# Six tiles instead of three held back at the stage borders of a two-block network, their weights kept in activation slots, and score products grouped by height

## The chip, the cores and the metric

One core of one Trainium2 chip runs the whole kernel in one launch. The metric is the device time in microseconds (us) of one execution; the lower the better. An engine's matmul is TensorE (PE); elementwise work lies on VectorE (DVE), ScalarE (ACT) and GpSimd (POOL); loads are issued on SyncE's queue (SP).

## The reference

The reference runs a first block of two layers (a mixer, attention to a memory, a convolutional feed-forward) on 512 tokens of width 1024, and then a second block of two layers. The change touches the second block only:

```python
for i in range(DEPTH):                       # layer 0 has a context stream of 256 tokens, layer 1 uses it only as input
    h  = modulate(rmsnorm(x, norm_mix_w[i]), sh_m, sc_m)
    hc = modulate(rmsnorm(ctx, norm_mix_w[i]), shc_m, scc_m)
    y, y_c = ab_mixer(h, hc, ...) if i % 2 == 0 else cd_mixer(h, hc, ...)
    x = x + g_m * y
    x = x + g_f * swiglu(modulate(rmsnorm(x, norm_ffn_w[i]), sh_f, sc_f), w_gate[i], w_up[i], w_down[i])
    if not last:
        ctx = ctx + gc_m * y_c
        ctx = ctx + gc_f * swiglu(modulate(rmsnorm(ctx, norm_ffn_w[i]), shc_f, scc_f), ...)
return rmsnorm(x, final_norm_w)
```

Here `modulate(h, shift, scale)` is `h * (1 + scale) + shift`. `cd_mixer` joins a Fourier mix with a gated linear attention of 4 heads that runs forward and backward over the tokens.

## The kernel before

Activations lie feature-major: a tile has 128 features by 512 tokens (256 for the context), eight tiles make the width of 1024. Every fp32 product is made of three products of reduced type: high weight by high activation, high by low, low by high. `unit` (L287 to L295) loads 128x1024 raw weights on SP (`wr`, 4 buffers), casts the high half on ACT (L293, `wh`, 3 buffers) and subtracts the low half on DVE (L294, `wl`, 3 buffers). Activations, squares and other working tiles come from one pool A of 66 slots through `T()`; PSUM has a pool for projections (`pm`, 4 banks) and one for the rest (`pa`, 4 banks).

The instructions are written down in program order, and a scheduler makes each engine's queue from that.

`gated` (L1421 on) is the output projection of a stage. For each of eight tiles m it takes the weights, makes x of the tile (three matmuls per 128 of depth), evacuates with gate and residual on DVE (L1428), and calls `stat_add` (L419 on): ACT squares the tile into a fresh slot of A (L423), and POOL adds it to a running sum (L428; DVE for the last tile). With a context it does the same with 256 tokens (evacuation L1438). Two things are held back at the border to the next stage, to give PE work there:

- `defer=3`: the context part of the last three tiles becomes six jobs (each half the depth). This is at border A (`w_abo`, layer 0 mixer to swiglu) and B (the third part of `w_dn0` to `cd_mixer`).
- `halves=3`: the last three x tiles are made in two halves of 256 tokens; the second halves become three jobs. This is at border C (`w_cdo` to swiglu, layer 1) and D (the third part of `w_dn1` to `final_norm`). Depth is 4 tiles of 128 at A and C, 6 at B and D.

The next stage runs the jobs and advances `modulate` between them: first the column sum of the squares (L417 on PE, L436 on DVE, L411 on POOL), later the broadcast (L480 on PE, L1089 on ACT). When all jobs have run, the eight tiles are modulated (L1102 on DVE, L1103 on ACT, L1110 on DVE; for three of them L1098 on POOL, L1099 and L1100 on ACT, L1108 on DVE), and the next projection begins (L1169, L1158). `cd_mixer` clears tiles by memset (L1549).

In `head` (L1758 on), for each of four heads and either direction, four score blocks are made of two products each: one of 128 rows (L1786, ZK by ZQ) and one of 64 rows (L1787, Z2), one after the other into the same block; a predicated copy then takes the bank of that direction. Other small products of the head have 64 rows too (L1774, L1776). A full fp32 product of 128 columns shows as two records.

Of the kernel before, what the change touches and what calls it, by code (L numbers as in the profile page):

```python
# [8 lines left out]
F32R = mybir.dt.float32r  # L9
# [141 lines left out]
def layout(i):  # L151
    a = {}
    a["x"] = fm_act(i["x"][0])
    a["mem"] = fm_act(i["mem"][0])
    v = {}
    for l in range(2):
        v[f"mixg{l}"] = cols(i["mix_norm_g"][l])
        v[f"xag{l}"] = cols(i["xa_norm_g"][l])
        v[f"xmg{l}"] = cols(i["xa_mem_norm_g"][l])
        v[f"ffg{l}"] = cols(i["ffn_norm_g"][l])  # L160
        v[f"xaq{l}"] = cols(i["xa_q_norm_g"][l])
        v[f"xak{l}"] = cols(i["xa_k_norm_g"][l])
        v[f"cw{l}"] = cols(i["ffn_conv_w"][l])
        v[f"cb{l}"] = cols(i["ffn_conv_b"][l])
        v[f"nm{l}"] = cols(i["norm_mix_w_2"][l])
        v[f"nf{l}"] = cols(i["norm_ffn_w_2"][l])
        v[f"ab{l}"] = cols(i["ada_b_2"][l])
    v["retg"] = cols(i["ev_ret_norm_g"][0])
    v["hgg"] = cols(i["ev_hg_norm_g"][0])
    v["lb"] = cols(i["hg_lb_logits"])  # L170
    v["odq"] = cols(i["od_q_norm_g"][0])
    v["odk"] = cols(i["od_k_norm_g"][0])
    v["nfin"] = cols(i["final_norm_w_2"])
    v["sgn"] = cols(i["ab_sgu_norm_w_2"][0])
    v["c"] = cols(i["c_2"][0])
    v["cc"] = cols(i["c_ctx_2"])
    v["dbf"] = cols(i["cd_decay_b_fwd_2"][0])
    v["dbb"] = cols(i["cd_decay_b_bwd_2"][0])
    v["hn"] = cols(i["cd_head_norm_w_2"][0])
    a["vec"] = np.ascontiguousarray(np.concatenate([v[n] for n, _ in VEC], axis=1))  # L180
    w = i["ev_w_in"][0]
    a["w_ev"] = fm_units(np.concatenate([w[:, 0:1024], w[:, 1536:3072], w[:, 3584:4096]], axis=1))
    a["w_evt"] = tm_units(np.concatenate([w[:, 1024:1536], w[:, 3072:3584]], axis=1))
    a["w_evo"] = fm_units(i["ev_w_out"][0])
    for l in range(2):
        a[f"w_xq{l}"] = fm_units(i["xa_w_q"][l])
        a[f"w_xk{l}"] = fm_units(i["xa_w_kv"][l][:, 0:1024])
        a[f"w_xv{l}"] = tm_units(i["xa_w_kv"][l][:, 1024:2048])
        a[f"w_xo{l}"] = fm_units(i["xa_w_o"][l])
        a[f"w_fi{l}"] = fm_units(i["ffn_w_in"][l])  # L190
        a[f"w_fo{l}"] = fm_units3(i["ffn_w_out"][l])
    a["w_od"] = fm_units(i["od_w_in"][0][:, 0:2048])
    a["w_odt"] = tm_units(i["od_w_in"][0][:, 2048:3072])
    a["w_odo"] = fm_units(i["od_w_out"][0])
    a["ctx"] = fm_act(i["ctx_2"][0])
    w = i["ab_w_in_2"][0]
    a["w_ab"] = fm_units(np.concatenate([w[:, 0:512], w[:, 1024:2048]], axis=1))
    a["w_abt"] = tm_units(np.concatenate([w[:, 512:1024], w[:, 2048:2560]], axis=1))
    a["w_abo"] = fm_units(i["ab_w_out_2"][0], 4)
    a["sguw"] = np.ascontiguousarray(i["ab_sgu_w_2"][0].transpose(2, 0, 1))  # L200
    a["sgub"] = np.ascontiguousarray(np.broadcast_to(i["ab_sgu_b_2"][0][None], (128, 4, 128)))
    q = np.arange(128)
    rel = np.arange(48) - 16
    ri = np.arange(8)[None, :, None] - (q // 16)[:, None, None] + 7
    ci = np.clip(rel[None, None, :] - (q % 16)[:, None, None] + 15, 0, 30)
    a["nab"] = np.ascontiguousarray(i["ab_rel_bias_2"][0][:, ri, ci].transpose(1, 0, 2, 3)).reshape(128, 8, 384)
    for l in range(2):
        a[f"w_gu{l}"] = fm_units(np.concatenate([i["ffn_w_gate_2"][l], i["ffn_w_up_2"][l]], axis=1))
        a[f"w_dn{l}"] = fm_units3(i["ffn_w_down_2"][l])
    a["w_ada"] = np.ascontiguousarray(i["ada_w_2"].reshape(2, 8, 128, 6, 2, 512).transpose(0, 3, 4, 1, 2, 5))  # L210
    w = i["cd_w_in_2"][0]
    z = np.zeros((1024, 16), np.float32)
    wa = np.concatenate([w[:, 2048:2064], z, w[:, 2064:2080], z, z, z, z, z], axis=1)
    a["w_cd"] = fm_units(np.concatenate([w[:, 512:1024], w[:, 1536:2048], wa, w[:, 0:512]], axis=1))
    a["w_cdt"] = tm_units(w[:, 1024:1536])
    a["w_cdo"] = fm_units(i["cd_w_out_2"][0], 4)
    dw = np.zeros((64, 512), np.float32)
    dw[0:16, 0:256], dw[16, 0:256] = i["cd_decay_w_fwd_2"][0], i["cd_decay_b_fwd_2"][0]
    dw[32:48, 256:512], dw[48, 256:512] = i["cd_decay_w_bwd_2"][0], i["cd_decay_b_bwd_2"][0]
    a["decw"] = dw  # L220
    dist = np.arange(128)[:, None] + 384 - np.arange(512)[None, :]
    a["odb"] = np.ascontiguousarray(i["rel_bias"][t5_bucket(dist)].transpose(2, 0, 1))
    return a


class Net:
# [917 lines left out]
    def wt(self, w, u, kt=8):  # L1144
        self.tick()
        return self.unit(self.a[w][u][:, 0:kt * 128])

    def dx(self, wt, xs, n=512, ps=None, s=None, ks=None):

        nc = self.nc  # L1150
        if ps is None:
            ps = self.PM()
        s = s or slice(0, n)
        last = len(xs) - 1
        for j in ks or range(last + 1):
            (xh, xl), ws = xs[j], slice(j * 128, j * 128 + 128)
            for i, (A, B) in enumerate(((wt[0], xh), (wt[0], xl), (wt[1], xh))):
                nc.tensor.matmul(ps[:, s], A[:, ws], B[:, s], start=j == 0 and i == 0, stop=j == last and i == 2)  # L1158
        return ps
# [87 lines left out]
    def ab_mixer(self, x, st, c, cs):  # L1247
        nc, a = self.nc, self.a
# [167 lines left out]
        jobs += [lambda m=m: out_part(m) for m in range(8)]  # L1416
        self.weave(units(), jobs, depth=4, rate=0.85)
        self.side = side
        return self.gated("w_abo", lambda m: 2 * m + 1, bx, bc, part, part_c, 0, 2, defer=3)

    def gated(self, w, u, yx, yc, x, c, l, j, defer=0, halves=0, stats=True):  # L1421

# [20 lines left out]
        whole = slice(0, 512)  # L1443
        held = []
        for m in range(8):
            wt = self.wt(w, u(m), len(yx))
            t = self.xp.tile([128, 512], F32, tag="x", name=f"x{self.n}") if m < 8 - halves else x[m]
            r["x"].append(t)
            if m < 8 - halves:
                ev_x(m, self.dx(wt, yx), t, whole)  # L1450
                if stats and halves:
                    for h, st in enumerate((r["sx"], r["sx2"])):
                        self.stat_add(st, m, t[:, h * 256:h * 256 + 256], 256)
                elif stats:
                    self.stat_add(r["sx"], m, t)
            else:
                held.append((m, wt, self.PM(), t))
            if yc:
                if m < 8 - defer:
                    self.run(part_c(m, wt))  # L1460
# [3 lines left out]
        for h, st in enumerate((r["sx"], r["sx2"])):  # L1464
            s = slice(h * 256, h * 256 + 256)

            def half(i, s=s, st=st):
                m, wt, ps, t = held[i]
                self.dx(wt, yx, 256, ps, s)
                ev_x(m, ps, t, s)  # L1470
                if stats:
                    self.stat_add(st, m, t[:, s], 256)

# [7 lines left out]
    def swiglu(self, l, r):  # L1481
# [9 lines left out]
            mx = self.modulate(x, r["sx"], l, 3, 0, xs, 256, H[0])  # L1491
        for i, job in enumerate(r["jobs"]):
            job()
            if i in ((2, 3) if c else (1, 2)):
                next(mx, None)
        self.run(mx)
        late = self.modulate(c, r["sc"], l, 3, 1, cs, 256, self.CS) if c else self.modulate(x, r["sx2"], l, 3, 0, xs, 256, H[1])
# [28 lines left out]
        for p, (lo, hi) in enumerate(PARTS):  # L1526
            for j in range(len(hx), min(hi + 1, 22)):
                gate_up(j)
            last = p == 2
            r = self.gated(f"w_dn{l}", lambda m: 3 * m + p, hx[lo:hi], hc[lo:hi], x, c, l, 5,  # L1530
                           defer=3 if last and c else 0, halves=3 if last and not c else 0, stats=last)
            x, c = r["x"], r["c"]
        return r

    def cd_mixer(self, r):
# [3 lines left out]
        mx = self.modulate(x, r["sx"], 1, 0, 0, xs)  # L1539
        for i, job in enumerate(r["jobs"]):  # L1540
            job()
            if i in (2, 3):
                next(mx, None)
        self.run(mx)
        SCf, SCb = self.T(), self.T()
# [211 lines left out]
        def head(h):  # L1757
# [20 lines left out]
            nc.scalar.copy(O1, p1)  # L1778
            nc.scalar.copy(O2[0], p2[0])
            nc.scalar.copy(O2[1], p2[1])  # L1780
            for d, SC in ((0, SCf), (1, SCb)):
                ZQ, ZK = Z[d]
                ps = self.PA()
                for j in range(4):
                    s = slice(j * 128, j * 128 + 128)
                    nc.tensor.matmul(ps[:, s], ZK[:, s], ZQ[:, s], start=True, stop=False)  # L1786
                    nc.tensor.matmul(ps[:, s], Z2[d][1][P, s], Z2[d][0][P, s], start=False, stop=True)  # L1787
                nc.vector.copy_predicated(SC.rearrange("p (b t) -> p b t", t=128), glm[:, d].bitcast(I32).unsqueeze(1).to_broadcast([128, 4, 128]),
                                          ps.rearrange("p (b t) -> p b t", t=128))
            SC = self.T()  # L1790
            nc.vector.tensor_add(SC, SCf, SCb)
            yield
# [44 lines left out]
            jobs += steps(f_out(g)) * 2  # L1837
        jobs += [lambda m=m: out_part(m) for m in range(8)]
        self.weave([head(0), head(1), decayed(1, 0), decayed(1, 1), head(2), head(3)], jobs, depth=2, rate=1.0)
        return self.gated("w_cdo", lambda m: 2 * m + 1, ys[4:8], None, part, None, 1, 2, halves=3)  # L1840

    def final_norm(self, r):
        nc = self.nc
# [20 lines left out]
                nc.sync.dma_start(self.a["out"][:, 2 * k:2 * k + 2, s], out[k].rearrange("p (k t) -> p k t", k=2))  # L1864

        first, second = half(0, r["sx"], 3), half(1, r["sx2"], 2)
        for job in r["jobs"]:
            job()
            next(first)
            if job is r["jobs"][1]:  # L1870
                break
        r["jobs"][2]()
        next(second)
        self.run(first, second)

# [123 lines left out]
```

## Time and profile before

| | |
|---|---|
| time of three runs, us | 3155.07, 3155.63, 3159.87 (median 3155.63) |
| the profiled execution, us | 3161.09 |
| its span, first to last instruction, us | 3159.3 |
| PE busy, us (share of the span) | 3102.5 (98%) |
| DVE, ACT, POOL busy, us | 1779.6, 1118.1, 436.7 |
| mean granted clock of TensorE | 0.991 |

The span is what the profile covers; the profiled execution has 1.8 us more around it. The share of busy time tells which engine has no room; the list of waits tells for what PE stood still; a timeline gives start, duration, engine, line and operation, and in brackets the idle time before and what ended it. The granted clock is given in windows as a share of full speed.

### The profile page before, as it was taken

How to read it: one execution, taken by the hardware profiler on the slowest of the kernel's cores; microseconds unless marked ns; L12 is line 12 of the kernel's file. 1: busy time of each engine (PE TensorE's matmuls, PEld its weight loads, DVE VectorE, ACT ScalarE, POOL GpSimd, SP SyncE). 2: the span in 40 equal slices, each digit the busy share in tenths (PEclk: the TensorE clock that was granted, in tenths of full speed). 3: DMA queues.
4: the chain of work that ended last, by engine and by line, in shares of the span. 5: the costliest groups of instructions: out<-in, count | busy, mean ns of one | idle time of the engine just before them, and what ended most of it. 6: DMA issues, size and time to landing. Idle time of an engine off the chain costs nothing. (4 is left out here: it accounts for less than half of the span.)

```text
span 3159.3 us, 40998 instructions
## 1 busy us (share of the span) xinstructions
PE 3102.5 (98%) x16292; PEld 2590.3 (82%) x16292; DVE 1779.6 (56%) x2894; ACT 1118.1 (35%) x1859; POOL 436.7 (14%) x375
## 2 busy tenths in 40 slices
PE   8999999999999999999999999999999999999998
PEld 6878888888877888888878778888888877788887
DVE  7767676575658857768654467342322453543333
ACT  2225353232445544423343545211212452342222
POOL 5023111010112111101121112000000310120001
PEclk9999999999999999999999999999999999999999
DMA  4224323333323423334342013232211220132222
GB/s 170 78 76 155 115 84 117 117 120 122 128 94 112 144 77 113 121 124 162 129 146 93 23 40 119 96 105 85 78 67 51 89 80 31 36 102 95 99 96 72
DMA packets 110355, 312.80 MB, mean 99 GB/s; under 512 B 12178, under 2 KB 17683, under 8 KB 110163
## 3 DMA queue, kind: packets, MB, share of 16 engines
q1 hardware_dynamic: 101968, 297.32, 27.7%
q10 hardware_dynamic: 8194, 12.86, 1.3%
q8 instruction: 128, 2.10, 0.3%
q14 instruction: 65, 0.52, 0.1%
HBM read 306.98 MB, written 3.15 MB: 98 GB/s over the span
## 5 line engine op out<-in xcount | busy, mean ns | idle before, releaser
L1158 PE MATMUL m<-t,wh 128*128 128x512 f32 (+1 forms) x4124 | 1093.0, 353 | 1.1 <-DVE t L1110 0.4
L293 ACT CAST wh<-wr 128x1024 fp32r<-128x1024 f32 (+2 forms) x485 | 487.8, 1008 | 1244.2 <-PE m L1158 422.2
L294 DVE TENSOR_TENSOR wl<-wr,wh 128x1024 fp32r<-128x1024 f32 (+2 forms) x485 | 579.2, 1195 | 450.1 <-ACT wh L293 438.3
L1158 PEld LDWEIGHTS m<-t,wh 128*128 128x128 f32 x4124 | 726.3, 190 | 115.3 <-issue 11.6
L312 PE MATMUL m<-t,wh 128*128 128x512 f32 (+1 forms) x2576 | 772.9, 383 | 0.0
L1158 PE MATMUL m<-t,wl 128*128 128x512 f32 (+1 forms) x2062 | 724.8, 352 | 0.5 <-DVE wl L294 0.5
L312 PEld LDWEIGHTS m<-t,wh 128*128 128x128 f32 x2576 | 474.1, 188 | 89.8 <-issue 1.0
L312 PE MATMUL m<-t,wl 128*128 128x512 f32 (+1 forms) x1288 | 491.5, 382 | 0.0
L1158 PEld LDWEIGHTS m<-t,wl 128*128 128x128 f32 x2062 | 390.8, 190 | 52.7 <-issue 1.9
L312 PEld LDWEIGHTS m<-t,wl 128*128 128x128 f32 x1288 | 242.7, 188 | 46.2 <-issue 0.7
L428 POOL TENSOR_TENSOR t<-t,t 128x512 f32<-128x512 f32 (+1 forms) x90 | 115.8, 1293 | 1162.8 <-ACT t L423 1162.4
L1062 DVE SCALAR_TENSOR_TENSOR t<-t,silc,t 128x512 f32<-128x512 f32 x280 | 219.0, 810 | 16.5 <-DMA t<-w_ada 15.8
L939 PE MATMUL m<-t,wh 128*128 128x512 f32 x704 | 217.3, 390 | 0.0
L342 PE MATMUL m<-t,wh 128*128 128x512 f32 x496 | 160.1, 402 | 7.3 <-ACT wh L293 7.3
L939 PEld LDWEIGHTS m<-t,wh 128*128 128x128 f32 x704 | 131.9, 188 | 27.2
L906 POOL TENSOR_TENSOR t<-t,t 128x512 f32<-128x512 f32 x44 | 64.5, 1465 | 549.8 <-ACT t L905 540.2
L401 ACT CAST t<-t 128x512 fp32r<-128x512 f32 x116 | 72.0, 621 | 189.0 <-DVE t L1520 104.0
L939 PE MATMUL m<-t,wl 128*128 128x512 f32 x352 | 137.1, 389 | 0.0
L1428 DVE SCALAR_TENSOR_TENSOR x<-m,modt,x 128x512 f32<-128x512 f32 (+1 forms) x70 | 49.3, 705 | 154.2 <-PE m L1158 154.1
L411 POOL TENSOR_TENSOR s<-s,nh 128x4 f32<-128x4 f32 (+2 forms) x67 | 72.1, 1078 | 439.3 <-DVE s L471 161.3
L357 PE MATMUL m<-wh,t 128*128 128x512 f32 x384 | 123.2, 397 | 0.0
L342 PEld LDWEIGHTS m<-t,wh 128*128 128x128 f32 x496 | 93.6, 192 | 26.7 <-ACT wh L293 8.0
(387 smaller groups left out, 3405.7 us busy)
## 6 DMA issues: line engine op xcount, KB each, us to landing
t<-w_ada SPq DMA_DIRECT2D x192, 256.0 KB, 4.0
wr<-w_fi SPq DMA_DIRECT2D x88, 512.0 KB, 3.3
wr<-w_gu SPq DMA_DIRECT2D x88, 512.0 KB, 3.3
wr<-w_fo SPq DMA_DIRECT2D x32, 512.0 KB, 3.4
wr<-w_dn SPq DMA_DIRECT2D x32, 512.0 KB, 3.2
wr<-w_ev SPq DMA_DIRECT2D x24, 512.0 KB, 3.3
wr<-w_xk SPq DMA_DIRECT2D x16, 512.0 KB, 3.4
wr<-w_xv SPq DMA_DIRECT2D x16, 512.0 KB, 3.4
```

Source lines behind the costliest of these rows:

```text
L293: nc.scalar.copy(h[:, 0:e], r[:, 0:e])
L294: nc.vector.tensor_sub(lo[:, 0:e], r[:, 0:e], h[:, 0:e])
L312: nc.tensor.matmul(ps[:, 0:n], A[:, s], B[:, 0:n], start=c == 0, stop=c == tot - 1)
L342: self.nc.tensor.matmul(ps, A[:, s], B, start=k == 0 and i == 0, stop=k == K - 1 and i == 2)
L357: nc.tensor.matmul(pss[tb], A[:, ts], B[:, s], start=(u == 0 and j == 0 and i == 0), stop=(u == nu - 1 and j == kper - 1 and i == 2))
L401: nc.scalar.copy(h[:, 0:n], src[:, 0:n])
L411: self.nc.gpsimd.tensor_tensor(r, v, self.nh[:, 0:w], ALU.pow)
L428: e.tensor_tensor(st[0][:, 0:n], st[0][:, 0:n], sq[:, 0:n], ALU.add)
L906: nc.gpsimd.tensor_tensor(y, y, rb, ALU.mult)
L939: nc.tensor.matmul(ps[:, 0:n], A[:, s], B[:, 0:n], start=c == 0, stop=c == tot - 1)
L1062: nc.vector.scalar_tensor_tensor(acc[i], r, s, acc[i], ALU.mult, ALU.add)
L1158: nc.tensor.matmul(ps[:, s], A[:, ws], B[:, s], start=j == 0 and i == 0, stop=j == last and i == 2)
```

## The change

- A class `Wide` joins several 512-wide pieces into one weight. `wt_kept` is a second way to take a weight: it casts and subtracts in pieces of 512 columns, high and low half of each piece into slots of A.
- In `gated`, tiles from 8 - max(defer, halves) on take their weights by `wt_kept`; held tiles no longer take a PSUM bank ahead.
- `defer` and `halves` rise from 3 to 6 (to 5 at border D); the places at which `modulate` is advanced between the jobs move back; `final_norm` advances its first half behind the first two jobs, runs the other three, and then takes the second half's statistics.
- In `head`, all products of 64 rows of both directions come first, then all of 128 rows, and then both copies; both PSUM banks are open meanwhile. Only a bank's first product starts it.

```diff
+class Wide:
+    def __init__(self, tiles):
+        self.tiles = tiles
+    def __getitem__(self, key):
+        s, o = key[1], key[1].start // 512
+        return self.tiles[o][key[0], s.start - o * 512:s.stop - o * 512]
...
+    def wt_kept(self, w, u, kt):
+        nc = self.nc
+        self.tick()
+        r = self.raw(self.a[w][u][:, 0:kt * 128])
+        hs, los = [], []
+        for o in range(0, kt * 128, 512):
+            n = min(512, kt * 128 - o)
+            h, lo = self.T(F32R), self.T(F32R)
+            nc.scalar.copy(h[:, 0:n], r[:, o:o + n])
+            nc.vector.tensor_sub(lo[:, 0:n], r[:, o:o + n], h[:, 0:n])
+            hs.append(h)
+            los.append(lo)
+        return Wide(hs), Wide(los)
...
-        return self.gated("w_abo", lambda m: 2 * m + 1, bx, bc, part, part_c, 0, 2, defer=3)
+        return self.gated("w_abo", lambda m: 2 * m + 1, bx, bc, part, part_c, 0, 2, defer=6)
...
         for m in range(8):
-            wt = self.wt(w, u(m), len(yx))
+            kept = m >= 8 - max(defer, halves)
+            wt = (self.wt_kept if kept else self.wt)(w, u(m), len(yx))
...
-                held.append((m, wt, self.PM(), t))
+                held.append((m, wt, t))
...
             def half(i, s=s, st=st):
-                m, wt, ps, t = held[i]
-                self.dx(wt, yx, 256, ps, s)
-                ev_x(m, ps, t, s)
+                m, wt, t = held[i]
+                ev_x(m, self.dx(wt, yx, 256, None, s), t, s)
...
-            if i in ((2, 3) if c else (1, 2)):
+            if i in ((4, 8) if c else (1, 3)):
                 next(mx, None)
...
-                           defer=3 if last and c else 0, halves=3 if last and not c else 0, stats=last)
+                           defer=6 if last and c else 0, halves=5 if last and not c else 0, stats=last)
...
-            if i in (2, 3):
+            if i in (2, 5):
                 next(mx, None)
...
-            for d, SC in ((0, SCf), (1, SCb)):
-                ZQ, ZK = Z[d]
-                ps = self.PA()
+            pss = [self.PA(), self.PA()]
+            for d in range(2):
                 for j in range(4):
                     s = slice(j * 128, j * 128 + 128)
-                    nc.tensor.matmul(ps[:, s], ZK[:, s], ZQ[:, s], start=True, stop=False)
-                    nc.tensor.matmul(ps[:, s], Z2[d][1][P, s], Z2[d][0][P, s], start=False, stop=True)
+                    nc.tensor.matmul(pss[d][:, s], Z2[d][1][P, s], Z2[d][0][P, s], start=j == 0, stop=False)
+            for d in range(2):
+                ZQ, ZK = Z[d]
+                for j in range(4):
+                    s = slice(j * 128, j * 128 + 128)
+                    nc.tensor.matmul(pss[d][:, s], ZK[:, s], ZQ[:, s], start=False, stop=j == 3)
+            for d, SC in ((0, SCf), (1, SCb)):
...
-        return self.gated("w_cdo", lambda m: 2 * m + 1, ys[4:8], None, part, None, 1, 2, halves=3)
+        return self.gated("w_cdo", lambda m: 2 * m + 1, ys[4:8], None, part, None, 1, 2, halves=6)
...
-        for job in r["jobs"]:
+        for i, job in enumerate(r["jobs"]):
             job()
-            next(first)
-            if job is r["jobs"][1]:
-                break
-        r["jobs"][2]()
+            if i < 2:
+                next(first)
         next(second)
```

## Rows read from the trace of the kernel before

**Rows 1.** The profile page: PE's busy time, share of the span and instructions, and the granted clock in 40 slices, in tenths of full speed (9 is 90% or more); last a group of DMA issues: name, instructions, KB each, median us from issue to landing.
```profile
PE 3102.5 (98%) x16292; PEld 2590.3 (82%) x16292; DVE 1779.6 (56%) x2894; ACT 1118.1 (35%) x1859; POOL 436.7 (14%) x375
...
PEclk9999999999999999999999999999999999999999
...
wr<-w_gu SPq DMA_DIRECT2D x88, 512.0 KB, 3.3
```

**Rows 2.** PE's waits: the waiting line and what released it, us in total, times, the longest.
```profile
PE a L417 <- DVE t L428: 11.3, 6, 2.5
...
PE a L480 <- POOL s L411: 7.1, 11, 1.3
```

**Rows 3.** Timeline of all engines at border A: start us, duration us, engine, line, operation, in brackets the idle time before and its releaser.
```profile
1930.73 0.63 ACT L423 ACTIVATE t<-x 128x512 f32<-128x512 f32 x1 [2.09 <-DVE x L1428]
...
1931.51 1.28 POOL L428 TENSOR_TENSOR t<-t,t 128x512 f32<-128x512 f32 x1 [1.43 <-ACT t L423]
...
1932.46 0.40 PE L1158 MATMUL m<-t,wh 128*128 128x256 f32 x2
...
1932.67 0.75 DVE L1428 SCALAR_TENSOR_TENSOR x<-m,modt,x 128x512 f32<-128x512 f32 x1 [1.97 <-PE m L1158]
...
1933.45 0.63 ACT L423 ACTIVATE t<-x 128x512 f32<-128x512 f32 x1 [2.09 <-DVE x L1428]
...
1937.96 0.65 PE L480 MATMUL a<-ident,s 128*128 128x128 f32 x4 [0.19 <-POOL s L411]
...
1941.17 0.98 PE L417 MATMUL a<-c,t 128*128 128x1 f32 x4 [2.32 <-DVE t L428]
```

**Rows 4.** Timeline of all engines at border B, columns as in the group before.
```profile
2496.43 0.65 PE L480 MATMUL a<-ident,s 128*128 128x128 f32 x4 [0.77 <-POOL s L411]
...
2498.91 0.48 DVE L1438 SCALAR_TENSOR_TENSOR c<-m,modt,c 128x256 f32<-128x256 f32 x1 [1.34 <-PE m L1158]
2499.31 0.74 DVE L1102 SCALAR_TENSOR_TENSOR t<-x,modt,a 128x512 f32<-128x512 f32 x1
2499.79 0.41 ACT L423 ACTIVATE t<-c 128x256 f32<-128x256 f32 x1
...
2500.87 0.58 PE L417 MATMUL a<-c,t 128*128 128x1 f32 x4 [2.00 <-DVE t L428]
...
2502.01 0.71 POOL L411 TENSOR_TENSOR s<-s,nh 128x2 f32<-128x2 f32 x1 [2.61 <-DVE s L436]
...
2502.77 0.43 PE L480 MATMUL a<-ident,s 128*128 128x128 f32 x2 [0.52 <-POOL s L411]
...
2506.02 4.73 POOL L1549 MEMSET t<- 128x512 f32 x10
```

**Rows 5.** Timeline of all engines at border C.
```profile
2779.13 0.43 PE L480 MATMUL a<-ident,s 128*128 128x128 f32 x2 [1.25 <-POOL s L411]
...
2781.83 0.99 PE L417 MATMUL a<-c,t 128*128 128x1 f32 x4 [2.27 <-DVE t L428]
...
2783.86 0.69 PE L480 MATMUL a<-ident,s 128*128 128x128 f32 x2 [1.04 <-POOL s L411]
```

**Rows 6.** Windows (from:to, length, then busy us and instructions of PE, PEld, DVE, ACT, POOL; then the granted clock, the share of the DMA engines and GB/s).
```profile
1940.50:1942.50 2.00, 1.33 (x5) 1.36 (x6) 1.87 (x4) 1.93 (x3) 0.15 (x2) 0.51 0.28 111
1942.50:1947.00 4.50, 4.50 (x13) 3.34 (x12) 4.50 (x6) 2.86 (x5) 3.99 (x3) 0.50 0.78 264
...
2503.80:2507.00 3.20, 3.20 (x9) 2.43 (x9) 3.20 (x4) 2.55 (x4) 3.20 (x5) 0.50 0.24 96
...
2780.20:2787.00 6.80, 4.13 (x19) 4.08 (x20) 4.64 (x12) 3.99 (x9) 3.71 (x5) 0.50 0.41 147
```

**Rows 7.** The chain of work that ended last, through the first pair of heads: start us, us, engine, bank, line and issues.
```profile
2643.80 0.64 PE a L1774 x4
...
2645.30 0.45 PE a L1774 x4
...
2646.61 0.42 PE a L1786 x2
2647.03 0.41 PE a L1787 x2
```

**Rows 8.** Timeline of all engines ahead of border C.
```profile
2765.94 0.62 ACT L293 CAST wh<-wr 128x512 fp32r<-128x512 f32 x1 [1.02 <-issue]
2766.13 0.75 DVE L1428 SCALAR_TENSOR_TENSOR x<-m,modt,x 128x512 f32<-128x512 f32 x1 [1.37 <-PE m L1158]
...
2766.91 0.73 ACT L423 ACTIVATE t<-x 128x256 f32<-128x256 f32 x2 [0.35 <-DVE x L1428]
```

**Rows 9.** The 512-wide cast of a weight (groups by line and shape: busy us, mean ns of one, idle before), and from the timeline of all engines ahead of border A the subtraction of the low half, first alone, then beside POOL's additions.
```profile
L293 ACT CAST wh<-wr 128x512 fp32r<-128x512 f32 x32 | 19.8, 620 | 48.4 <-PE m L1158 39.1 <-issue 9.3
...
1908.82 0.69 DVE L294 TENSOR_TENSOR wl<-wr,wh 128x512 fp32r<-128x512 f32 x1
...
1916.25 2.44 POOL L428 TENSOR_TENSOR t<-t,t 128x512 f32<-128x512 f32 x2 [1.81 <-ACT t L423]
...
1916.69 1.40 DVE L294 TENSOR_TENSOR wl<-wr,wh 128x512 fp32r<-128x512 f32 x1
```

**Rows 10.** The chain of work that ended last: a dense stretch of 96 matmuls of 512 columns, and one of 18 matmuls of 256 columns.
```profile
2622.04 21.76 PE m L1158 x96
...
3146.30 2.15 PE m L1158 x18
```

More of the change, by code (lines that the diff above doesn't have):

```diff
@@ L1780, in head @@
             nc.scalar.copy(O2[1], p2[1])
-            for d, SC in ((0, SCf), (1, SCb)):
-                ZQ, ZK = Z[d]
-                ps = self.PA()
+            pss = [self.PA(), self.PA()]
+            for d in range(2):
                 for j in range(4):
                     s = slice(j * 128, j * 128 + 128)
-                    nc.tensor.matmul(ps[:, s], ZK[:, s], ZQ[:, s], start=True, stop=False)
-                    nc.tensor.matmul(ps[:, s], Z2[d][1][P, s], Z2[d][0][P, s], start=False, stop=True)
+                    nc.tensor.matmul(pss[d][:, s], Z2[d][1][P, s], Z2[d][0][P, s], start=j == 0, stop=False)
[5 more added lines that the diff above has]
+            for d, SC in ((0, SCf), (1, SCb)):
                 nc.vector.copy_predicated(SC.rearrange("p (b t) -> p b t", t=128), glm[:, d].bitcast(I32).unsqueeze(1).to_broadcast([128, 4, 128]),
-                                          ps.rearrange("p (b t) -> p b t", t=128))
+                                          pss[d].rearrange("p (b t) -> p b t", t=128))
             SC = self.T()
```

## The prediction, made blind

> **What bounds the kernel now.** I read the profile page first: TensorE (PE) is busy 98% of the span and the line of granted clocks shows full speed in all 40 slices [rows 1]. So a change pays only where it shortens PE's own work or one of its few waits. The list of PE's waits says where these are [rows 2]: most for the column sum L417 after the addition of squares L428 (11.3 us in 6 waits), 7.1 us for the broadcast L480 after POOL's rsqrt. These are the stage borders. Third I read the timelines of the borders, called A (mixer to swiglu, layer 0), B (swiglu to cd_mixer), C (cd_mixer to swiglu) and D (the end). At A, PE waits 0.19 us at L480 and 2.32 at L417 [rows 3]; at B 0.77, 2.00 and 0.52 [rows 4]; at C 1.25, 2.27 and 1.04 [rows 5]. Fourth, the windows: the granted clock is 0.50 (the 1.2 GHz level) in 4.5, 3.2 and 4.13 busy us behind A, B and C [rows 6]; half of each is lost, 2.25, 1.6 and 2.1 us. Last the chain through the score products [rows 7].
>
> **In which order tiles are written.** The step that decides is the change's choice of place: the kept weights are cast into slots of the activation pool A, which also holds the squares of L423. Now a weight has pools of its own and its cast runs ahead: at C the 512-wide cast L293 starts at 2765.94, before the evacuation L1428 (2766.13) and the square (2766.91) of an earlier tile [rows 8]. Slots of A, by contrast, seem to be written first in the program's order. At B the broadcast was ready at 2497.08 and DVE idled 1.34 us, yet the first modulate L1102 starts at 2499.31, only behind the last deferred L1438; the memsets L1549, which read nothing, start at 2506.02, though POOL had no work for 2.61 us before its L411 at 2502.01 [rows 4]. I take it that this order holds for the new casts too. In the changed program the square of tile m is written before the weights of tile m+1. At A and B the cast of each kept x tile then waits for the square of the tile before, that for its evacuation, that for the last matmul: no weight is prefetched across tiles. The held tiles become six, and PE stands still ahead of each.
>
> **Parts at A and B.** From the end of PE's last issue for a tile to the evacuation 0.21 us (1932.46 to 1932.67), to the square 0.78, the square 0.63 [rows 3], the 512-wide cast 0.62 [rows 9], a hand-over of some 0.05 (an estimate): 2.3 us. Two matmuls with the high half follow (0.454 us at 21.76/96 = 0.227 each [rows 10]); the third needs the low half. Its subtraction takes 0.69 alone, but 1.40 beside POOL's addition of squares [rows 9]; that starts 0.15 us behind the square [rows 3] and lasts 1.2 to 1.3, so it lies beside most of the subtraction. The excess over the 0.454 is 0.28 to 1.0, and I take 0.8, nearer the second row: 3.1 us a tile. The first kept tile follows a context tile (0.48 and 0.41 us in place of 0.75 and 0.63 [rows 3, 4]): 2.6. Border A: 5 x 3.1 + 2.6 = 18.1; B the same, since its second, narrower piece is cast beside the first's matmuls. Together **+36.2 us**, from 2 x (5 x 2.58 + 2.1) = 30.0 to 2 x (5 x 3.3 + 2.8) = 38.6.
>
> Behind the waiting casts ACT has only later casts and that tile's square, DVE the subtraction and the next evacuation, and nobody else needs them. The raw loads on SP keep their number and order, but a raw buffer comes free one tile later and the next stage's loads with it; twelve deferred context jobs (six issues of 0.12 us each at A, nine at B [rows 10]) cover these, and without that cover a load would cost up to its time to landing, 3.3 us [rows 1]. The casts in pieces cost a little more ACT and DVE time, off the path.
>
> **What the borders give back.** Twelve jobs instead of six, with the broadcast four or five jobs after the sum, cover the waits at L480 (0.19 and 0.77). The end stays: the last context square still goes through L428 and L417 behind the last job, and the modulate cannot pass the last L1438. Of the waits of 2.0 to 2.3 us there I count half as filled by modulate work that stands ready earlier: -1.6 at A, -1.3 at B, **-2.9**. Bounds: nothing, and all of them (0.19 + 2.32 + 0.77 + 2.00 + 0.52 = 5.8).
>
> **C and D.** Here all held weights are cast one behind the other, with no square between them, so there is one stall each of 3.0 us (before the first held tile); the three more tiles in halves at C and two at D cost, per matmul, 2.15/18 = 0.119 instead of 0.227/2 [rows 10], 0.4 us more at either border. At C the six second halves cover most of the three waits (4.56): -3.4, from 0 to -4.6. C sums to **0**, D to +3.0 + 0.4 - 0.2 = **+3.2**: its tail, the last stat, rsqrt and store, has the same steps as before.
>
> **Score products.** Now 64-row and 128-row products alternate. Two L1786 issues take 0.42 us, two L1787 0.41; four L1774 behind a 64-row group take 0.45, so two 0.225; behind a 128-row group 0.64 [rows 7]. Each change of height costs 0.19. Per pair of heads there are 34 changes now (one in, 32 between products, one out), four after: 30 x 0.19 = 5.8, and for two pairs **-11.5 us**, from -9 (some of it back in waits for the later copy) to -12. The second PSUM bank is held a little longer; the 16 products of a head together take 16 x 0.225 = 3.6 us, no wait for a bank is in the rows, so I cost it at nothing.
>
> **The clock.** Twelve stalls of about 3 us between 2.7 us (A, 12 matmuls) and 4.1 us (B, 18) of work. At A the clock fell to 0.51 in a stretch that holds the wait of 2.32 [rows 3, 6], so these stalls can do it as well. One low stretch cost 1.6 to 2.25, mean 2.0: 12 x 2.0 = 24, less 0.45 for each stall, since two slow matmuls cover more of the subtraction: **+18 us**. Bounds: nothing, and every kept matmul at the half level, 6 x 2.7 + 6 x 4.1 - 5.4 = 35. The Trainium skill (TensorE: Matmul & The Clock Gate, HAM oscillation) names a length of gap below which the array should keep its clock; by it none of these stalls would lower it and the sum would stay at 25. The row at A speaks against: its wait was shorter than these and the clock fell.
>
> **Sum**: 36.2 - 2.9 + 0 + 3.2 - 11.5 = +25.0, and 18 of clock: +43. The profiled execution took 3161.1 us (span 3159.3, 1.8 around it), 5.5 above the median of the runs, so it would be 3204; from the median, 3155.6 + 43 = **3199 us**.
>
> **The rivals.** (1) Ends on the other side: the casts run ahead as today. Its place is the order of first writes in A; from the point where a cast may start before the square of the tile before, there is no stall at A to D. Then the borders give back their waits with the low clock behind them: A 2.3 + 2.25, B 3.3 + 1.6, C 4.0 less 0.4, D about 0.3 lost; with the heads -11.5 that is 24 us faster: **3131**. For it: the slots are not scarce, and nothing in the data makes a cast wait. Against: the memsets and the modulate at B. Chance 0.10. (2) Gated, but stalls at the lower bound and no loss of clock: 30.0 - 2.9 + 3.2 - 11.5 = 18.8: **3174**; for it that the granted clock is full in nearly all of the kernel. Chance 0.14. (3) Gated, and the clock stays low through all kept tiles: 25 + 35 = 60: **3216**; for it that stall follows stall with less than 4.1 us of work between them. Chance 0.16. (4) The change does little, stalls and gains in balance, for instance if only the gated cast but not the subtraction is waited for and ACT is early: within 6 us of before, 0.03. My forecast, between 3185 and 3210, has 0.57.
>
> **How the numbers follow.** What a measurement can tell from no change is 0.2%, 6.3 us. Only rival 1 is faster by more: 0.10. Same 0.03, slower 0.87. The range leaves out rival 1 and the outer edge of rival 3, and takes in rival 2 with a smaller stall: 3166 to 3222.
>
> **What would show it.** In the changed profile: at A and B each first matmul of a kept tile waits for a cast or a subtraction of `wt_kept`, about 2.3 to 3.3 us, six times each; each such cast starts as the square of the tile before ends; a granted clock well under 1 in both stretches. PE's waits at L480 gone at A and B, the last L417 still there. L1786 and L1787 in their new grouping at 0.11 us an issue. One stall of about 3 us at C and at D. I am wrong if casts of `wt_kept` start before the squares of the earlier tile, or if PE's idle time at A and B does not rise by some 30 us; then rival 1 holds and the time is below 3145.

## The result and the profile after

The changed kernel takes 3207.39 us (median of four runs, 3201.94 to 3208.2) against 3157.75 for the kernel before: ratio 1.0149, 95% interval 1.0136 to 1.0162, so 47 us slower (about 43 to 51); the two medians differ by 49.6, and the median of the kernel before now includes a fourth run of 3160.95 us. The forecast was 3199 in a range of 3166 to 3222. The profiled execution took 3206.59 us with a span of 3204.8.

Line numbers have moved: the evacuation L1428 is now L1453, the square L423 is L433, the addition L428 is L438, the column sum L417 is L427, the broadcast L480 is L490, the projection L1158 is L1183. The new casts of kept weights are L1167, their subtractions L1168. First the page, PE's busy time and the granted clock in 40 slices [rows 1], then the list of PE's waits [rows 2]: waiting line and releaser, us in total, times, longest.

```profile
PE 3115.4 (97%) x16364; PEld 2600.6 (81%) x16364; DVE 1788.5 (56%) x2910; ACT 1118.9 (35%) x1870; POOL 432.4 (13%) x375
...
PEclk9999999999999999999999998999999899999999
```

```profile
PE m L1183 <- ACT t L1167: 27.4, 14, 2.1
PE a L427 <- DVE t L438: 10.0, 7, 2.5
PE m L1183 <- DVE t L1168: 8.7, 13, 1.9
...
PE a L490 <- POOL s L421: 4.9, 9, 1.2
```

Two new waits stand in the list, on the casts and on the subtractions of kept weights: 36.1 us together. The old ones have become less by only 1.3 and 2.2 us (11.3 to 10.0, 7.1 to 4.9). Now the timeline of all engines at border A, one kept tile to the next:

```profile
1915.62 0.75 DVE L1453 SCALAR_TENSOR_TENSOR x<-m,modt,x 128x512 f32<-128x512 f32 x1 [2.00 <-PE m L1183]
1916.40 0.63 ACT L433 ACTIVATE t<-x 128x512 f32<-128x512 f32 x1 [4.57 <-DVE x L1453]
1916.94 0.60 ACT L1167 CAST t<-wr 128x512 fp32r<-128x512 f32 x1
1917.17 1.27 POOL L438 TENSOR_TENSOR t<-t,t 128x512 f32<-128x512 f32 x1 [4.76 <-ACT t L433]
1917.57 1.43 DVE L1168 TENSOR_TENSOR t<-wr,t 128x512 fp32r<-128x512 f32 x1 [1.20 <-ACT t L1167]
1917.59 0.73 PE L1183 MATMUL m<-t,t 128*128 128x512 f32 x2 [2.01 <-ACT t L1167]
...
1919.05 4.14 PE L1183 MATMUL m<-t,t 128*128 128x512 f32 x10 [0.73 <-DVE t L1168]
```

This is the chain that was forecast, step by step: evacuation, square, cast right behind the square, PE after 2.01 us of standing still; two matmuls; then 0.73 us more for the subtraction, which takes 1.43 us beside POOL's addition, against 0.69 alone [rows 9]. The Trainium skill (SBUF — State Buffer, Who interferes with whom) says that a VectorE instruction with two SBUF inputs contends with a GpSimd instruction that reads SBUF; the trace agrees, 1.43 against 0.69. The ten matmuls behind it take 4.14 us where 2.27 would be dense (10 x 0.227 [rows 10]): the clock is low, 0.75 of full speed on average over the kept tiles of A (a window of that stretch stands below, at the run with three kept tiles). At B the same, with one subtraction later still because it stands in DVE's queue behind two of the next stage's:

```profile
2500.53 0.73 PE L1183 MATMUL m<-t,t 128*128 128x512 f32 x2 [2.01 <-ACT t L1167]
2502.00 5.54 PE L1183 MATMUL m<-t,t 128*128 128x512 f32 x16 [0.73 <-DVE t L1168]
...
2522.50 6.01 PE L1183 MATMUL m<-t,t 128*128 128x512 f32 x16 [1.91 <-DVE t L1168]
```

To see where the time went, the kernel is cut at instructions that both kernels have: stage A from the last cast (L1350, now L1375) of layer 0's attention to its eighth gate activation of the swiglu; B from the last such activation to the first gate of `cd_mixer`; C, with the heads in it, from the last of these gates to the eighth activation of layer 1's swiglu; D from the last activation to the end. Between the stages both kernels take the same time to 0.02 us. Windows A, B, D and C of the kernel before (columns as in [rows 6]):

```profile
1905.19:2067.62 162.43, 159.92 (x914) 140.29 (x915) 87.69 (x130) 55.94 (x93) 23.65 (x20) 0.98 0.29 103
2435.36:2629.65 194.29, 188.01 (x957) 155.32 (x956) 94.12 (x157) 83.18 (x126) 43.30 (x45) 0.96 0.23 78
3109.61:3159.30 49.69, 39.87 (x232) 35.03 (x230) 20.15 (x35) 15.00 (x32) 14.21 (x19) 0.93 0.19 67
...
2644.14:2870.47 226.33, 220.62 (x1208) 179.84 (x1207) 108.40 (x192) 79.12 (x140) 29.57 (x34) 0.98 0.19 61
```

and of the changed kernel:

```profile
1903.63:2091.78 188.15, 170.97 (x914) 144.58 (x915) 90.27 (x131) 56.63 (x93) 20.91 (x20) 0.93 0.26 89
2459.52:2677.23 217.71, 196.47 (x957) 158.22 (x956) 99.28 (x163) 83.77 (x132) 40.94 (x45) 0.94 0.21 69
3148.84:3204.80 55.96, 43.57 (x268) 39.57 (x266) 21.13 (x42) 15.24 (x37) 14.00 (x19) 0.89 0.17 59
...
2691.71:2909.69 217.98, 211.85 (x1244) 179.37 (x1243) 109.17 (x195) 78.63 (x139) 28.88 (x34) 0.98 0.20 63
```

A has grown by 25.7 us, B by 23.4, D by 6.3; C has shrunk by 8.35. The sum is 47.1; less the 1.6 us by which the changed kernel reached stage A earlier, it is the difference of the spans, 45.5. At A and B the growth falls into two parts: PE stands still longer (2.5 to 17.2 us at A, 6.3 to 21.2 at B) and is busy longer with the same count of matmuls (159.9 to 171.0, 188.0 to 196.5).

The heads, in the chain that ended last [rows 7]; L1810 are the 64-row products, L1815 those of 128 rows:

```profile
2692.88 0.44 PE a L1799 x4
...
2694.19 1.78 PE a L1810 x16
2695.97 1.98 PE a L1815 x16
2697.95 0.64 PE a L1799 x4
```

Sixteen issues take 1.78 us, 0.111 each, where two took 0.42. One change of height (0.2 us) is left inside the group, one behind it.

### The profile page after: what moved, and what is told of

The parts are those of the page before. It is cut to its first block, busy times and chain, and to the rows that moved or that the text cites. A ratio compares the mean times of both kernels' runs of the same rounds, so it can differ in the third digit from the quotient of the medians.

```text
span 3204.8 us, 41143 instructions
## 1 busy us (share of the span) xinstructions
PE 3115.4 (97%) x16364; PEld 2600.6 (81%) x16364; DVE 1788.5 (56%) x2910; ACT 1118.9 (35%) x1870; POOL 432.4 (13%) x375
## 3 DMA queue, kind: packets, MB, share of 16 engines
q8 instruction: 129, 2.11, 0.3%
## 5 line engine op out<-in xcount | busy, mean ns | idle before, releaser
L1183 PE MATMUL m<-t,wh 128*128 128x512 f32 (+1 forms) x3716 | 995.4, 355 | 1.1 <-DVE t L1120 0.3
L303 ACT CAST wh<-wr 128x1024 fp32r<-128x1024 f32 (+2 forms) x462 | 471.2, 1022 | 1218.4 <-PE m L1183 402.9
L304 DVE TENSOR_TENSOR wl<-wr,wh 128x1024 fp32r<-128x1024 f32 (+2 forms) x462 | 559.1, 1211 | 445.7 <-ACT wh L303 429.9
L322 PE MATMUL m<-t,wh 128*128 128x512 f32 (+1 forms) x2576 | 772.1, 382 | 0.0
L1183 PEld LDWEIGHTS m<-t,wh 128*128 128x128 f32 x3716 | 656.1, 189 | 107.5 <-issue 11.2
L1183 PE MATMUL m<-t,wl 128*128 128x512 f32 (+1 forms) x1858 | 656.8, 354 | 0.5 <-DVE wl L304 0.5
L322 PEld LDWEIGHTS m<-t,wh 128*128 128x128 f32 x2576 | 473.9, 188 | 89.5 <-issue 1.0
L322 PE MATMUL m<-t,wl 128*128 128x512 f32 (+1 forms) x1288 | 491.0, 381 | 0.0
L1183 PEld LDWEIGHTS m<-t,wl 128*128 128x128 f32 x1858 | 351.6, 189 | 49.7 <-issue 1.9
L322 PEld LDWEIGHTS m<-t,wl 128*128 128x128 f32 x1288 | 242.6, 188 | 46.3 <-issue 0.7
L438 POOL TENSOR_TENSOR t<-t,t 128x512 f32<-128x512 f32 (+1 forms) x90 | 111.1, 1236 | 1229.9 <-ACT t L433 1229.3
L1183 PE MATMUL m<-t,t 128*128 128x256 f32 (+1 forms) x684 | 132.7, 355 | 36.2 <-ACT t L1167 27.4
L1183 PEld LDWEIGHTS m<-t,t 128*128 128x128 f32 x684 | 109.5, 217 | 58.4 <-ACT t L1167 33.8
L1453 DVE SCALAR_TENSOR_TENSOR x<-m,modt,x 128x512 f32<-128x512 f32 (+1 forms) x75 | 50.3, 672 | 188.9 <-PE m L1183 188.9
L949 PEld LDWEIGHTS m<-t,wh 128*128 128x128 f32 x704 | 131.8, 188 | 27.2
```

The source lines that it names most:

```text
L303: nc.scalar.copy(h[:, 0:e], r[:, 0:e])
L304: nc.vector.tensor_sub(lo[:, 0:e], r[:, 0:e], h[:, 0:e])
L322: nc.tensor.matmul(ps[:, 0:n], A[:, s], B[:, 0:n], start=c == 0, stop=c == tot - 1)
L438: e.tensor_tensor(st[0][:, 0:n], st[0][:, 0:n], sq[:, 0:n], ALU.add)
L949: nc.tensor.matmul(ps[:, 0:n], A[:, s], B[:, 0:n], start=c == 0, stop=c == tot - 1)
L1453: nc.vector.scalar_tensor_tensor(t[:, s], px[:, s], self.M(l, j, 0, m), x[m][:, s], ALU.mult, ALU.add)
```

## The experiments

All runs beside runs of the kernel before; ratios with 95% intervals. The theory to be tested: the kept casts stand behind the squares because both write slots of one pool in program order, PE stands still for each kept tile, and its clock falls. The rivals: the raw weights arrive late, and the casts in pieces and six held tiles cost time by themselves.

**The score products alone** (the new block of `head` in the kernel before).

> The kernel before with the grouped score products alone. If the 11 us that the changed kernel gained over the heads belong to the changes of row height, this gains the same with nothing else altered: 3157.8 - 11.5 = about 3146 us (3144 to 3149). If they came from something else in the change (other buffers, other order around the heads), it stays within 3 us of before.

Measured 3147.87 us, ratio 0.9964 (0.9954 to 0.9974); in a second run, below, 0.9971. Stage C went from 226.33 to 215.27 us, A, B and D stayed within 1.1 us. So the 11 us belong to the new block of `head`, and all the rest of the change costs 58 us by the ratios. That within the block it is the heights rests on their price: 60 changes fewer at the 0.2 us seen at L1799 (0.64 against 0.44) are 12 us. The block also changes the banks and which product starts one; no run changes these alone.

**Weights one tile earlier in the program.**

```diff
-            kept = m >= 8 - max(defer, halves)
-            wt = (self.wt_kept if kept else self.wt)(w, u(m), len(yx))
+            wt = nxt if nxt is not None else take(m)
+            nxt = take(m + 1) if 7 - max(defer, halves) <= m < 7 else None
```

> The changed kernel, but each kept tile's weights are taken one tile earlier in the program, so before the square of the tile ahead of it; slots, pieces, deferral and score products as in the changed kernel. Order theory (the cast stands behind the square because both write slots of one pool in program order): the stalls go at B, C and D; at A about 0.5 us a tile is left, because cast and subtraction then stand behind the square of one tile before and end about 3.7 us after a tile's start, against 3.2 us at which the low half is wanted. Time 3146 + 3 + up to 5: 3145 to 3155. Late-load theory (the raw weights arrive late): loads are issued at most one tile earlier, some gain, about 3180. Work theory (casts in pieces and six held tiles cost by themselves): unchanged, about 3205.

Measured 3153.78, ratio 0.9982 (0.9973 to 0.9992). A took 165.0 us instead of 188.2, B 192.8 instead of 217.7. What is left at A, PE's timeline:

```profile
1910.98 3.01 PE L1183 MATMUL m<-t,t 128*128 128x512 f32 x12 [0.30 <-DVE t L1168]
1914.29 3.08 PE L1183 MATMUL m<-t,t 128*128 128x512 f32 x12 [0.30 <-DVE t L1168]
1918.81 3.04 PE L1183 MATMUL m<-t,t 128*128 128x512 f32 x12 [1.44 <-DVE t L1168]
1922.31 6.18 PE L1183 MATMUL m<-t,t 128*128 128x512 f32 x40 [0.46 <-DVE t L1168]
```

Two of the six kept tiles wait for nothing, and four for 0.30 to 1.44 us where 1.9 to 2.7 stood, and these on the subtraction, as expected; at B one wait of 0.57 us is left. At C the expectation missed: the stall shrank from 2.42 to 0.88 us, but the wait at the column sum L427 grew from 0.30 to 1.70, and the stage took 218.1 us as before the edit (218.0). At A and B order alone takes nearly all of the stalls away. A want of slots is no rival either: these weights take as many slots of A as in the changed kernel, and take them earlier. But loads also go out earlier here; the next run keeps their place in the program.

**Squares in a buffer of their own at A and B.** Weights, squares and evacuations stay where they are in the program.

```diff
+        self.sq = E(tc.tile_pool(name="sq", bufs=1))
...
+        if own and k:
+            sq = self.sq.tile([128, 512], F32, tag="q", name=f"q{self.n}")
+        else:
+            sq = self.T()
...
-                self.stat_add(r["sc"], m, t, 256)
+                self.stat_add(r["sc"], m, t, 256, own=defer > 0)
...
-                    self.stat_add(r["sx"], m, t)
+                    self.stat_add(r["sx"], m, t, own=defer > 0)
```

> The changed kernel with one edit: at the borders A and B the squares get a buffer of their own outside the pool; the weights stay in the pool's slots, and the program's order of weights, evacuations and squares stays too. Order theory: casts run ahead again at A and B, all twelve stalls and the low clock there go (about 50 us), C and D keep theirs (about 9 us together): 3150 to 3158. Late-load theory and work theory: nothing changes, 3200 to 3210.

Measured 3151.65, ratio 0.9975 (0.9965 to 0.9984): 55 us less than the changed kernel, by the ratios and by the medians. A 163.4, B 188.2; D, which kept its squares in the pool, 53.3, and C 218.6. ACT's timeline at A (L438 is the square now, L1172 the kept cast):

```profile
1910.89 0.63 ACT L438 ACTIVATE q<-x 128x512 f32<-128x512 f32 x1 [1.56 <-DVE x L1458]
1911.43 0.60 ACT L1172 CAST t<-wr 128x512 fp32r<-128x512 f32 x1
...
1912.93 0.42 ACT L438 ACTIVATE q<-c 128x256 f32<-128x256 f32 x1 [0.90 <-POOL t L443]
1913.26 1.12 ACT L1172 CAST t<-wr 128x512 fp32r<-128x512 f32 x2
...
1916.68 0.63 ACT L438 ACTIVATE q<-x 128x512 f32<-128x512 f32 x1 [2.30 <-DVE x L1458]
```

Two casts now follow each other before the next square: they run ahead, from the same raw loads. Both rivals fall: neither the place of the loads in the program nor the extra work had been changed.

**Three kept tiles.** `defer` and `halves` back to 3, with `wt_kept` for these three; the steps of `modulate` stand where the kernel before has them.

> The changed kernel with three tiles held at every border as before, their weights still in the pool's slots, score products grouped. Order theory: three stalls each at A and B instead of six, half of the 50 us, one each at C and D: 3146 + 25 + 6 = about 3177 (3170 to 3185). Late-load theory: three raw buffers come free in time, no stall: about 3147. Work theory: the pieces cost little for three tiles, 3146 to 3152.

Measured 3187.3, ratio 1.0089 (1.0068 to 1.011). The direction is that of the order theory, but 2 us above its bounds. The four times are 3181.99, 3182.45, 3192.15 and 3192.71 us, and the profile is of the third: two lie inside the bounds, and what follows holds for one execution of the longer two. At A PE stood still 10.3 us and at B 12.6 (17.2 and 21.2 with six tiles, 2.5 and 6.3 before), so that has about halved. But it was busy 168.3 and 196.3 us, nearly as long as with six. Windows from the end of work ahead of the first stall to the column sum of x, A and B with three kept tiles, then with six:

```profile
1927.75:1953.72 25.97, 18.11 (x60) 13.08 (x60) 12.17 (x13) 5.96 (x11) 5.68 (x5) 0.74 0.46 156
2497.31:2528.79 31.48, 24.06 (x82) 18.20 (x82) 10.05 (x13) 5.70 (x12) 4.68 (x4) 0.73 0.21 67
...
1910.35:1957.43 47.08, 32.42 (x103) 22.66 (x103) 20.92 (x24) 10.53 (x18) 9.08 (x8) 0.75 0.41 134
2483.22:2538.61 55.39, 39.20 (x136) 28.60 (x137) 19.88 (x24) 12.27 (x23) 8.14 (x7) 0.82 0.24 81
```

What the granted clock lacks of full speed, times the length of the window, is an estimate of the clock lost: 6.8 us at A with three kept tiles and 11.8 with six, 8.5 and 10.0 at B. At A the loss in the kept tiles goes with the number of stalls; at B three cost most of what six do. More clock was lost behind the kept tiles of A, around the waits on the sums: 0.96 granted over the rest of the stage with three kept tiles, 0.99 with six.

**Idle work in the stalls.** Ahead of each kept tile at A and B three fp32 matmuls of the last x tile into an unread bank:

```diff
+            if defer and kept:
+                fill = self.PA()
+                for _ in range(3):
+                    nc.tensor.matmul(fill[:, 0:256], self.ident, r["x"][m - 1][:, 0:256], start=True, stop=True)
```

> The changed kernel with idle work for TensorE: ahead of each of the twelve kept tiles at A and B, three fp32 matmuls of 256 columns (0.48 us each) of the x tile just evacuated, into a bank that nobody reads. The stalls stay (the cast still stands behind the square), but most of each is filled. If the low clock in the kept tiles (PE busy about 10 us longer at A and 10 at B than before, with the same count of matmuls) comes from the stalls, it stays high: 15 to 20 us less, less up to 0.4 us a tile for the filling: 3185 to 3195. If the clock fell for another reason, the time is that of the changed kernel or a few us more, 3205 to 3215.

Measured 3193.96, ratio 1.0117 (1.0102 to 1.0133), 13 us less than the changed kernel by the medians and 10 by the ratios, though PE does more. The stall is still there, now half filled by L1478 (0.84 and 0.61 us are left of 2.74), and the subtraction still ends it (PE's timeline, then window A):

```profile
1915.83 1.56 PE L1478 MATMUL a<-x,ident 128*128 128x256 f32 x6 [0.84 <-DVE x L1453]
1917.04 0.81 PE L1183 MATMUL m<-t,t 128*128 128x512 f32 x2
1918.47 2.59 PE L1183 MATMUL m<-t,t 128*128 128x512 f32 x10 [0.61 <-DVE t L1168]
```

```profile
1903.03:2082.93 179.90, 169.56 (x950) 145.14 (x951) 90.20 (x131) 56.77 (x93) 20.91 (x20) 0.99 0.27 93
```

Ten matmuls take 2.59 us instead of 4.14, the granted clock of stage A is 0.99 instead of 0.93, and the stage takes 179.9 instead of 188.2. So the stalls had caused the low clock of A, and it cost at least these 8.3 us beside the standing still. At B the gain was 3.2 us only (214.5), with a granted clock of 0.96 for 0.94; 0.96 is also that of the kernel before.

**All squares out of the pool**, at C and D too (`own=True` at each call).

> The changed kernel with all squares of these borders in a buffer of their own, at C and D too. Order theory: the stalls of 2.4 to 2.9 us at C and D go as well, with the low clock behind D's: 3151.7 of the run with A and B alone, less 2 to 6: 3146 to 3150. If one buffer for squares holds POOL and ACT up where two squares follow a tile (C and D), it is 3150 or more.

Measured 3140.76, ratio 0.9945 (0.9932 to 0.9959); once more beside the last run:

> All four borders wide, all their squares in a buffer of their own, on the same chip as the run before it: 0.9945 of before, 3139 to 3143.

3139.98, ratio 0.9936 (0.9923 to 0.995). D is back at 50.1 us, C at 212.3, 2.9 below the run of the heads alone; the first of the two runs was better than expected by 5 us. So with all squares apart the change is worth 7 to 9 us over the heads alone, by the medians; what part of this the six held tiles have is taken up next.

**Where it is worth it.**

> The score products grouped, and the six-tile border at B alone, its squares in a buffer of their own; A, C and D hold three tiles as before, in the weights' own pools. By the stages of the earlier runs, B without stalls took 188.2 us against 193.3 with three tiles held: 5 us less than the run of the heads alone, 3142 to 3144 beside 3147 to 3148. If the 5 us came from elsewhere, no difference from heads.

Measured 3142.77, ratio 0.995 (0.9937 to 0.9962); the heads alone beside it:

> The kernel before with grouped score products again, for the comparison on one chip with the run before it: 0.9964 of before, 3146 to 3149 us.

3148.84, ratio 0.9971 (0.9958 to 0.9983). Stage B took 188.1 us against 193.7. The wait at the column sum L428, 2.00 us in [rows 4], has gone from B, one at the broadcast is left (PE's timeline of the run with squares apart, B then A):

```profile
2512.11 0.43 PE L495 MATMUL a<-ident,s 128*128 128x128 f32 x2 [1.39 <-POOL s L422]
```

```profile
1932.59 1.02 PE L428 MATMUL a<-c,t 128*128 128x1 f32 x8 [1.15 <-DVE t L443]
...
1943.47 0.58 PE L428 MATMUL a<-c,t 128*128 128x1 f32 x4 [1.76 <-DVE t L443]
```

At A two waits on the sums are left, 2.9 us in sum against 2.5 at the border before [rows 3], and nothing is gained. The squares there wait for POOL's addition to free their one buffer, and so the column sum comes late; a second buffer was not tried:

```profile
1931.09 0.63 ACT L438 ACTIVATE q<-x 128x512 f32<-128x512 f32 x1 [1.40 <-POOL t L443]
```

The traces also show where the gain at B comes from. In the run with the weights one tile earlier six tiles are held as well, but the squares stay in the pool, and B took 192.8 us, hardly less than with the heads alone (193.3). There the first modulate (L1112) starts behind the last deferred evacuation (L1463), as in [rows 4], long after the copy of the broadcast (L1099). With the squares apart (last line, L1117) it starts right behind that copy, and the deferred evacuations go on until 2498.38:

```profile
2488.08 0.57 ACT L1099 COPY t<-a 128x512 f32<-128x512 f32 x1
...
2494.14 0.48 DVE L1463 SCALAR_TENSOR_TENSOR c<-m,modt,c 128x256 f32<-128x256 f32 x1 [1.67 <-PE m L1183]
...
2494.54 0.74 DVE L1112 SCALAR_TENSOR_TENSOR t<-x,modt,a 128x512 f32<-128x512 f32 x1
...
2492.53 0.75 DVE L1117 SCALAR_TENSOR_TENSOR t<-x,modt,a 128x512 f32<-128x512 f32 x1 [0.57 <-ACT t L1104]
```

So the buffer for the squares frees the modulate as well as the casts, and six held tiles without it gained next to nothing at B. Whether three held tiles with the squares apart would gain as much is not shown: no run has that. With six held tiles and squares apart at B and C alone:

> Wide borders only where the stages of the earlier runs show a gain: six tiles held at B (188.2 us against 193.5) and C (212.3 against 215.2), their squares in a buffer of their own; A (163.5 against 162.05) and D hold three tiles in the old way; score products grouped. If stages add up, 1.5 us less than the run with all four borders wide: 3138 to 3141, ratio to before 0.993 to 0.995. If a stage's gain depends on the others, up to 3145.

3139.57, ratio 0.9939 (0.9927 to 0.9952), not to be told from all four borders, which ran beside it. Stages A and D, 162.1 and 49.9 us, stand as in the kernel before.

## Why the prediction was right, point by point

- **Order of first writes**: right. Casts start as the square ends, in each of the kept tiles at A and B; with the squares elsewhere they run ahead. This was inferred from memsets and a modulate that waited without a need [rows 4]; the run with squares apart shows it.
- **The stalls at A and B**: forecast 36.2 us, PE stood still 14.6 at A and 16.1 at B on L1167 and L1168. The chain was right, its size 5.5 us too large. Of the 0.21 us from the last issue to the evacuation 0.17 are counted as busy in the trace, since a matmul's record runs to its end (12 x 0.17 = 2.0 of the difference). The first kept tile waited 1.9 and 1.5 us instead of 2.6. In later stalls the low clock covered more of the subtraction (0.24 to 0.39 us in place of 0.73), which I had put under the clock, while the late subtraction at B went the other way (1.91).
- **The clock**: forecast 18 us, mainly at A and B. PE is busy 11.0 and 8.5 us longer there, 17.5 in sum without the 2.0 us of ends; filling gave 11.5 back at the two and cost up to 0.4 a tile. The rule of the Trainium skill that I weighed (TensorE: Matmul & The Clock Gate, HAM oscillation) would have left the clock up at stalls of this length; the trace disagrees, in stalls of 2.01 and 0.73 us. A fixed loss for each stall fits A with three tiles (6.8 us against 11.8) and not B (8.5 against 10.0), so that the sum came out so close is in part luck.
- **The borders' gain** of 2.9: the step failed. At A the waits are 2.07 and 0.46 us, in sum as before [rows 3]; at B 1.66 and 0.47, 1.2 less than [rows 4]. The modulate work that was to fill them did not stand ready earlier: it waited for the last deferred evacuation, as the prediction itself says of it. (Half of the waits in the rows is 1.3 at A and 1.6 at B; the prediction has the two the other way round, and its sum stands.)

```profile
1966.00 0.58 PE L427 MATMUL a<-c,t 128*128 128x1 f32 x4 [2.07 <-DVE t L438]
1967.62 0.69 PE L490 MATMUL a<-ident,s 128*128 128x128 f32 x2 [0.46 <-POOL s L421]
```

- **C and D**: forecast 0 and +3.2, measured 217.98 - 215.27 = +2.7 (against the heads alone) and +6.3. The stall at C was 2.10 + 0.32 us, that at D 2.11 + 0.80, where 3.0 were forecast for each. At C the gain was mis-sized: waits of 0.30, 1.65 and 0.58 are left of 4.56 us [rows 5], 2.0 less, not 3.4; and PE was busy 2.3 us longer, where 0.4 had been counted. At D I had counted no loss of clock: 106 issues took 15.68 us, 0.148 each, where 0.119 is dense [rows 10], 3.0 us. The run with the squares apart at A and B has the same program and the same stall at D, and there they took 12.97 us (third line); why the clock fell in the one execution and not in the other is open.

```profile
3168.03 0.50 PE L1183 MATMUL m<-t,t 128*128 128x256 f32 x2 [2.11 <-ACT t L1167]
...
3169.32 15.68 PE L1183 MATMUL m<-t,t 128*128 128x256 f32 x106 [0.80 <-DVE t L1168]
...
3116.78 12.97 PE L1188 MATMUL m<-t,t 128*128 128x256 f32 x106 [0.79 <-DVE t L1173]
```

- **The heads**: forecast -11.5, measured -11.1.

Put together: at A and B 36.2 + 18 - 2.9 = 51.3 us were forecast and 49.1 measured (32.7 of stalls with the ends, 17.5 of clock, 1.1 of gain), at C (without the heads) and D 3.2 and 9.0. The largest errors are the stalls at A and B, 3.5 us too many with the ends, and the missing clock at D, 3.0 too few; they point in opposite ways, so the total is nearer than its terms. The rival that ends faster priced what a version without stalls would give at 3131; measured 3140, mostly because A gives nothing back: 163.1 us against 162.4 before, where 4.6 less had been counted.

Open: what more than one buffer for the squares would give at A, why filling gained less at B, and what six held tiles are worth beside three with the squares apart.

## What to carry to other kernels

Before a tile is put into another pool, look at what else writes to that pool between its place in the program and the place where it is wanted: one shared pool chained an early cast, and the modulate too, to the latest of these, while the same number of slots taken earlier in the program did no harm. A buffer of its own for the small, short-lived tile (here one of 2 KB a partition) undid 55 us at A and B. When an edit frees two things at once, run each alone before the gain is put down to one of them. Price a stall on a busy TensorE with its clock as well.

## What was not expected of the hardware

The same stall of 2.1 + 0.8 us at D was followed by 106 matmuls in 15.68 us in one execution and in 12.97 in another. The clock lost in the kept tiles did not simply follow the number of stalls: with three it was 6.8 us at A and 8.5 at B, with six 11.8 and 10.0 (estimates from the windows above, three stalls in one execution only). Idle matmuls in the gaps were worth their time: 11.5 us less at A and B with 72 more issues.
